# A fifth pair of split-weight buffers in place of two load buffers, and twelve unread products behind the router's logits

## The chip, the cores and the metric
The program runs on one core of one Trainium2 chip. The metric is the time of one execution on the device in microseconds (us). The engines that matter here are TensorE (PE in the profile; its weight loads are a row of their own, PEld), VectorE (DVE), ScalarE (ACT) and the queue of SyncE (SPq) that issues every transfer.

## The reference, cut to what matters
A trunk of two layers over 256 tokens of width 1024, all in float32. Layer 0 is a retention block and a dense SwiGLU block, layer 1 a pooling mixer and a block of eight experts. The change touches the way from the mixer through the router into the experts:

```python
logits = (xt @ w_router).astype(jnp.float32)
top_logits, top_idx = lax.top_k(logits, TOP_K)          # two of eight experts for each token
gates = jax.nn.softmax(top_logits, axis=-1)
...
(jax.nn.silu(h @ w_gate) * (h @ w_up)) @ w_down         # each expert: 1024 -> 3584 -> 1024
```

All eight experts' weights are read, 336 MiB in float32, whatever the router chooses.

## The kernel before, in words
Activations and weights stay in float32. A product is made from parts: a weight tile `w` is split into `w_hi` (the value rounded to float32r, written by ACT) and `w_lo` (the rest, `w - w_hi`, written by DVE), both by `split` at L118. An activation is split the same way. `mm3` (L166 to L168) adds three products of parts, `mm2` (L778, L779) two, for experts whose tokens fit in half a tile and whose activation parts lie side by side ("narrow" experts; the three "wide" ones use `mm3`).

**The tiles of weights.** A weight part is a tile of 128 x 2048 float32, 1 MiB. `load` (L144) takes the next load buffer from a ring of tags and issues one transfer on SyncE's queue. `halves_of` takes the next pair of buffers for `w_hi` and `w_lo`. A load buffer is free again when DVE has written `w_lo`; a pair is free again when PE has used it. Before the experts the kernel has three pairs. From the pool mixer on, a fourth is made of two buffers that served other tiles (tags `cb` and `T_l`). The ring in the experts' loop has six buffers of tag `raw` and four of tag `e8`; the `e8` buffers held `xT` and the four `yT` tiles of the retention block before, and join the ring at the start of the dense block. Two more (`SPARE`) help for a few loads at the start.

**The experts' loop.** Each expert has seven blocks of 512 hidden columns. `BLOCKS` puts the blocks of expert 0 first and mixes wide and narrow ones after that, three wide in each seven. `PROGRAM` lists the steps: for each block gate (`g`), up (`u`) and, two blocks later, down (`d`). A step uses two weight tiles, its first half the first and its second half the second: 24 products of 128 x 512 for a wide block, 16 for a narrow one. The loop stands inside `tc.manual_schedule()`: every engine gets its instructions in the order in which they are written. In that order each step splits two more tiles (`fetch`, one behind the step's products and one behind the small steps that follow), so that `AHEAD` tiles are split before their step:

```python
while len(stream) < AHEAD:
    fetch()
for n, (what, block) in enumerate(PROGRAM):
    ...
    ps = up(next_weights(), ready[p][0], not wide)
    fetch()
    ...
    step()
    fetch()
```

The split that stands behind a step's first half of products writes the pair which that half has just used, so ACT (and DVE behind it) waits there for PE. With every expert's last block come `scaled` (DVE, `y_g`, L848), `upper` (ACT, `yp`, L853), `lower` (DVE, `yp`, L858) and four products `give` (PE, L867) with an addition each (DVE, `xs`, L872); `give` and the gathers for the next expert (`prepare`, L753) write to two banks of PSUM (`tbank`) and wait for DVE to empty them.

**In front of the loop.** The router's logits are the last products of the mixer (L580). From them DVE makes `sel` (L602), PE three small sums (L648 to L650), DVE `slot` and the one-hot tiles `oh` (L730); PE gathers the first expert's tokens (L753), and ACT and DVE split them into `xe_n`. Only then can PE multiply by the first weights (L778).

Of the kernel before, what the change touches and what calls it, by code (L numbers as in the profile page):

```python
# [11 lines left out]
R = mybir.dt.float32r  # L12
# [7 lines left out]
P = 128  # L20
D = 1024
KD = D // P
T = 256
# [6 lines left out]
NE = 8  # L30
# [12 lines left out]

W_FIRST = (8, 4, 0, 2)
W_REST = (5, 9, 1, 3, 6, 10, 7, 11)
N_RAW, N_SPL, N_E8, N_OHT = 6, 3, 4, 4


HALF = P // 2
# [8 lines left out]
PROGRAM = [("d", BLOCKS[i - 2]) if what == "d" else (what, BLOCKS[i]) for i in range(NE * NJ + 2) for what in "gud"  # L58
           if (i > 1 if what == "d" else i < NE * NJ)]

AHEAD = 4
ALWAYS = math.inf

SPARE = ((8, "a8", 2, 2), (11, "kd", 1, 3))
# [5 lines left out]
def trunk(ctx, tc, x, cols, c_row, const, ada_0, ada, w_0, w_in, w_out, f_gu, f_dn, pool_w, m_g, m_u, m_d, out):  # L70
    nc = tc.nc
# [9 lines left out]
    def tbank():  # L81
        return psT.tile([P, 512], F, tag="t", name="tbank")

    def buf(tag, shape, bufs=1, dt=F, name=None):
        return act.tile([P] + shape, dt, tag=tag, name=name or tag, bufs=bufs)
# [24 lines left out]
    cb = buf("cb", [2048])[:, :D]  # L110
    silu_c = nc.scalar.activation(c1, c1, AF.Silu)
    for h in range(2):
        ps = tbank()
# [6 lines left out]
    @contextmanager  # L120
    def behind(*instructions):

        with ExitStack() as s:
            for i in instructions:
                s.enter_context(tc.issue_after(i.ins))
            yield


    ring = deque([("raw", N_RAW, ALWAYS)] * N_RAW)
    halves = deque([("w_hi", "w_lo", N_SPL)] * N_SPL)  # L130
# [138 lines left out]
    def tok(b):  # L269
        return slice(b * P, (b + 1) * P)  # L270
# [7 lines left out]
        normed(xn, b)  # L278
    hh, hl = hT_parts()
    a1 = cst.tile([P, KD], F, name="a1")  # L280
    xT = buf("e8", [KD, T], N_E8, name="xT")
    for b in range(TB):
        for g in range(0, KD, 4):
            ps = transpose4(xn[:, b, g * P:(g + 4) * P])
# [4 lines left out]
    for k in range(KD):  # L289
# [6 lines left out]
        for f in range(4):  # L296
            wh, wl = at(512 * f)
# [50 lines left out]
    def attend(h, st):  # L348
        s, vy = st[f"s{h}"], st[f"vy{h}"]
        v, y = vy[:, 0], vy[:, 1]  # L350
        yT = st[f"yT{h}"] = buf("e8", [2, 4, T], N_E8, R, name="yT")
        os = []
        mv = sm.tile([P, TB, 2], F, tag="mv", name="mv")
        for b in range(TB):
            o = bank()
            nc.tensor.matmul(o, s[:, tok(b)], v[:, 0], start=True, stop=(b == 0))
            if b:
                nc.tensor.matmul(o, s[:, 256:384], v[:, 1], start=False, stop=True)
            bn = sm.tile([P, 6], F, tag="bn", name="bn")
            nc.vector.bn_stats(bn, o)  # L360
            nc.vector.bn_aggr(mv[:, b], bn)
            nc.vector.scalar_tensor_tensor(y[:, b], o, mv[:, b, 0:1], y[:, b], op0=ALU.subtract, op1=ALU.mult)
        rs, _ = rstd_of(mv[:, :, 1], 1.0, TB)
        for b in range(TB):
            nc.scalar.activation(y[:, b], y[:, b], AF.Copy, scale=rs[:, b:b + 1])
            ps = transpose4(y[:, b])
            for i in range(4):
                gain = col[:, C_GN + 4 * h + i:C_GN + 4 * h + i + 1]
                p1, hi = ps[:, i * P:(i + 1) * P], yT[:, 0, i, tok(b)]
                nc.scalar.activation(hi, p1, AF.Copy, scale=gain)  # L370
                nc.vector.scalar_tensor_tensor(yT[:, 1, i, tok(b)], p1, gain, hi.bitcast(F),
                                               op0=ALU.mult, op1=ALU.subtract)
# [7 lines left out]
    st = {}  # L380
# [5 lines left out]
    for i, f in enumerate(W_REST):  # L386
        at = weights(w_in[i])
        pss = [bank() for _ in range(TB)]
        for k in range(KD):
            wh, wl = at(512 * k)  # L390
# [8 lines left out]
    for h in range(NH):  # L399
        yT = st[f"yT{h}"]  # L400
        at = weights(w_out[h])
        last = h == NH - 1
# [3 lines left out]
        for i, b in steps:  # L406
            for n in range(2):
                wh, wl = at(1024 * i + 512 * n)
# [1 line left out]
        ada_next(ADA_O[h])  # L410


    ring.extend([("e8", N_E8, ALWAYS)] * N_E8)
    xn = buf("a8", [TB, D], 2, name="xn")
    hh, hl = hT_parts()
    a = acol(0, 3, gain_of(0, 1))
# [2 lines left out]
    for b in range(TB):  # L419
        root, scaled, _ = normed(xn, b)  # L420
# [8 lines left out]
        for g in range(0, KD, 4):  # L429
            ps = transpose4(xn[:, b, g * P:(g + 4) * P])  # L430
            for i in range(4):
                k = g + i
# [38 lines left out]
    for j in range(NFB):  # L471
# [8 lines left out]
        if j == 7:  # L480
# [5 lines left out]
            r = buf("qk", [2, D], name="pool_rows")  # L486
            gs_row, gsb_row = row(r[:, 0], gs), row(r[:, 1], gsb)
            a_p, s_p = acol(1, 0, gain_of(1, 0)), mcol(1, 0)
        if j == 9:
# [4 lines left out]
            rt = cst.tile([P, KD, NE], F, name="rt")  # L494
            nc.vector.tensor_mul(rt, rt0, a_m.rearrange("p (k o) -> p k o", o=1).to_broadcast([P, KD, NE]))
            ps = tbank()
            for k in range(KD):
                nc.tensor.matmul(ps[:, 0:NE], s_m[:, k:k + 1].to_broadcast([P, P]), rt0[:, k],
                                 start=(k == 0), stop=(k == KD - 1))
# [3 lines left out]
    last = [(NFB - 2, down_weights(NFB - 2), th)]  # L503
# [8 lines left out]
    for b in range(TB):  # L512
        for j, at, th in last:
            for c in range(2):
                down_block(j, at, th, c, b)


    xn = buf("T_l", [TB, D], name="xn_p")
    hT = buf("a8", [TB, KD, P], 2, name="hT_p")
# [8 lines left out]
    r = buf("raw", [2, D], N_RAW, name="m_rows")  # L528
# [3 lines left out]
    xT = []  # L532
# [17 lines left out]
    for b in range(TB):  # L550
        pooled = [bank() for _ in range(2)]
        for g in range(0, KD, 4):
            ps = transpose4(xn[:, b, g * P:(g + 4) * P])
# [6 lines left out]
        for n in range(2):  # L560
            ps = bank()
# [14 lines left out]
    for b in range(TB):  # L576
        rs, root = norm_scale(b, lambda n: w2([512], "junk"))
        ps = tbank()
        for k in range(KD):
            nc.tensor.matmul(ps[:, 0:NE], xT[b][:, k], rt[:, k], start=(k == 0), stop=(k == KD - 1))  # L580
        nc.vector.scalar_tensor_tensor(lg[:, b], ps[:, 0:NE], rs, lg0, op0=ALU.mult, op1=ALU.add)
        if b == 0:

            for c in (slice(0, 512), slice(512, 1024)):
                nc.vector.scalar_tensor_tensor(xm[:, b, c], xm[:, b, c], rs, sm_row[:, c], op0=ALU.mult, op1=ALU.add)
# [31 lines left out]

    halves.append(("cb", "T_l", 1))  # L620
    once = [ring[i][:2] + (1,) for i in range(2)]
    ring.rotate(-2)
    for place, *spare in SPARE:
# [13 lines left out]
    def next_weights():  # L637
# [4 lines left out]
            return hi[:, c % 2048:c % 2048 + n], lo[:, c % 2048:c % 2048 + n]  # L642
        return at


    ps = tbank()
    tri = kp[:, K_TRI:K_TRI + P]
# [282 lines left out]
    with tc.manual_schedule():  # L930
# [3 lines that stand above are left out]
# [17 lines left out]
            else:  # L951
# [3 lines left out]
                ps = up(next_weights(), ready[p][0], not wide)  # L955
# [25 lines left out]
    place_i, _, room, most_i = known  # L981
# [120 lines left out]
```

## Time and profile before

| | us |
|---|---|
| median of three executions | 1387.05 (1383.2 to 1388.51) |
| the profiled execution, its own time | 1383.0 |
| the span of its profile | 1381.0 |
| PE busy in it | 1307.7 (95%) |
| DVE busy | 1214.6 (88%) |
| ACT busy | 957.5 (69%) |

The page counts an engine as busy while one of its instructions runs. Matmuls are pipelined and their ends are modelled: a product of 512 columns counts 0.39 us though the next one may start 0.23 us after it. So a gap in PE's busy time is a real stall, while a stall of less than 0.17 us is not seen as one. "Idle before" with a name behind an arrow is the time in which the engine stood still and what released it.

### The profile page before, as it was taken

The numbers are of one execution on the slowest core, as the hardware profiler recorded it, in microseconds if no ns is written. First come the engines' busy times: TensorE is split into PE (matmuls) and PEld (weight loads), VectorE is DVE, ScalarE is ACT, GpSimd is POOL, SyncE is SP. The second block draws the span as 40 slices with busy tenths as digits, with TensorE's granted clock in tenths as the row PEclk, the third lists the DMA queues.
The fourth block names the chain that finished last, engine by engine and source line by source line (L and its number), as shares of the span: only waits on it lengthen the run. The fifth ranks groups of instructions, "written<-read, shape, count | busy, mean of one in ns | idle before, by whom it ended". The sixth has DMA issues, their size and how long they took to land.

```text
span 1381.0 us, 16731 instructions
## 1 busy us (share of the span) xinstructions
PE 1307.7 (95%) x6142; PEld 1067.0 (77%) x6142; DVE 1214.6 (88%) x1119; ACT 957.5 (69%) x888; POOL 0.2 (0%) x4
## 2 busy tenths in 40 slices
PE   7999998999998889999999999999999999999994
PEld 5787877888887768877878877788778787878883
DVE  6889866998766799999989999999899889999994
ACT  6655455443436588877878887878877877878882
POOL 0000000000000000000000000000000000000000
PEclk9999999999999799999999999999999999999997
DMA  9977885898770999999999999999999999999950
GB/s 389 361 279 259 324 291 208 336 393 352 289 327 31 340 350 389 360 374 392 425 411 395 426 394 363 387 397 406 409 357 421 355 376 376 380 398 401 426 245 33
DMA packets 66474, 477.30 MB, mean 346 GB/s; under 512 B 7377, under 2 KB 7761, under 8 KB 8658
## 3 DMA queue, kind: packets, MB, share of 16 engines
q1 hardware_dynamic: 66386, 476.17, 87.9%
q8 instruction: 50, 0.82, 0.2%
q14 instruction: 38, 0.31, 0.1%
HBM read 475.10 MB, written 1.05 MB: 345 GB/s over the span
## 4 chain that ended last, share of the span: by engine, by line
PE 42%; DVE 13%; issue 7%; ACT 3%; DVEq 0%; ACTq 0%
DVE w_lo L118 10%; PE bank L779 8%; PE bank L778 8%; PE bank L166 7%; PE bank L167 7%; PE bank L168 6%; PE tbank L818 3%; ACT w_hi L118 2%; PE tbank L753 2%; PE tbank L867 1%; DVE xs L872 1%; DVE dT L118 1%; DVE yp L858 1%; DVE y_g L848 0%; DVE moe_h L798 0%
## 5 line engine op out<-in xcount | busy, mean ns | idle before, releaser
L118 DVE TENSOR_TENSOR w_lo<-raw,w_hi 128x2048 fp32r<-128x2048 f32 (+1 forms) x413 | 904.9, 2223 | 99.4 <-ACT w_hi L118 97.8
L118 ACT ACTIVATE w_hi<-raw 128x2048 fp32r<-128x2048 f32 (+1 forms) x413 | 757.8, 1864 | 188.8 <-PE bank L168 139.6
L779 PE MATMUL bank<-w_lo,xe_n 128*128 128x512 f32 x560 | 223.6, 399 | 6.7 <-DVE w_lo L118 5.7
L778 PE MATMUL bank<-w_hi,xe_n 128*128 128x512 f32 x560 | 224.5, 401 | 0.3 <-ACT w_hi L118 0.3
L166 PE MATMUL bank<-w_hi,T_h 128*128 128x512 f32 x352 | 141.3, 403 | 3.1 <-ACT T_h L118 3.1
L167 PE MATMUL bank<-w_lo,T_h 128*128 128x512 f32 x352 | 139.3, 396 | 2.4 <-DVE w_lo L118 2.4
L168 PE MATMUL bank<-w_hi,T_l 128*128 128x512 f32 x352 | 139.5, 397 | 0.5 <-DVE T_l L118 0.5
L779 PEld LDWEIGHTS bank<-w_lo,xe_n 128*128 128x128 f32 x560 | 106.8, 191 | 35.9 <-DVE w_lo L118 14.4
L166 PE MATMUL bank<-w_hi,xe 128*128 128x512 f32 x336 | 132.8, 395 | 0.0
L167 PE MATMUL bank<-w_lo,xe 128*128 128x512 f32 x336 | 131.8, 392 | 0.4
L168 PE MATMUL bank<-w_hi,xe 128*128 128x512 f32 x336 | 131.1, 390 | 0.0
L778 PEld LDWEIGHTS bank<-w_hi,xe_n 128*128 128x128 f32 x560 | 106.9, 191 | 22.2 <-ACT w_hi L118 0.8
L779 PE MATMUL bank<-w_lo,dT 128*128 128x512 f32 x280 | 112.3, 401 | 8.2 <-DVE w_lo L118 8.2
L778 PE MATMUL bank<-w_hi,dT 128*128 128x512 f32 x280 | 111.6, 398 | 6.4 <-DVE dT L118 6.4
L177 DVE SCALAR_TENSOR_TENSOR raw<-raw,cb 128x1024 f32<-128x1024 f32 x96 | 114.3, 1217 | 0.1
L166 PE MATMUL bank<-w_hi,dT 128*128 128x512 f32 x256 | 100.0, 391 | 0.0
L167 PE MATMUL bank<-w_lo,dT 128*128 128x512 f32 x256 | 99.7, 390 | 0.0
L168 PE MATMUL bank<-w_hi,dT 128*128 128x512 f32 x256 | 99.7, 390 | 0.0
L166 PEld LDWEIGHTS bank<-w_hi,T_h 128*128 128x128 f32 x352 | 67.2, 191 | 17.7 <-ACT T_h L118 3.8
L167 PEld LDWEIGHTS bank<-w_lo,T_h 128*128 128x128 f32 x352 | 67.1, 191 | 16.8 <-DVE w_lo L118 2.8
L168 PEld LDWEIGHTS bank<-w_hi,T_l 128*128 128x128 f32 x352 | 67.1, 190 | 15.2 <-DVE T_l L118 1.2
L167 PEld LDWEIGHTS bank<-w_lo,xe 128*128 128x128 f32 x336 | 63.1, 188 | 16.2 <-DVE w_lo L118 3.7
(227 smaller groups left out, 1415.0 us busy)
## 6 DMA issues: line engine op xcount, KB each, us to landing
raw<-in_m_g_dram SPq DMA_DIRECT2D x112, 1024.0 KB, 7.6
raw<-in_m_u_dram SPq DMA_DIRECT2D x112, 1024.0 KB, 7.6
raw<-in_m_d_dram SPq DMA_DIRECT2D x112, 1024.0 KB, 7.5
raw<-in_ada_dram SPq DMA_DIRECT2D x48, 1024.0 KB, 7.1
raw<-in_f_gu_dram SPq DMA_DIRECT2D x22, 1024.0 KB, 5.8
raw<-in_w_in_dram SPq DMA_DIRECT2D x16, 1024.0 KB, 5.1
raw<-in_f_dn_dram SPq DMA_DIRECT2D x11, 1024.0 KB, 6.9
raw<-in_w_dram SPq DMA_DIRECT2D x8, 1024.0 KB, 7.7
```

The source lines that it names most:

```text
L118: return nc.scalar.activation(hi, src, AF.Copy), nc.vector.tensor_sub(lo, src, hi.bitcast(F))
L166: nc.tensor.matmul(ps, xh, wh, start=start, stop=False)
L167: nc.tensor.matmul(ps, xh, wl, start=False, stop=False)
L168: nc.tensor.matmul(ps, xl, wh, start=False, stop=stop)
L177: nc.vector.scalar_tensor_tensor(s, s, 1.0, cb, op0=ALU.mult, op1=ALU.mult, accum_out=mod[:, m:m + 1])
L753: nc.tensor.matmul(ps[:, i * ns:(i + 1) * ns], xm[:, b, c], oh[:, b, 0:ns], start=(b == 0), stop=(b == TB - 1))
L778: nc.tensor.matmul(ps, x, wh, start=start, stop=False)
L779: nc.tensor.matmul(ps, x, wl, start=False, stop=stop)
L818: nc.tensor.matmul(ps[:, i, c], a[:, c * P:(c + 1) * P], fold, start=True, stop=True)
L858: nc.vector.tensor_sub(yp[:, 1, half(n)], y_g[:, half(n)], yp[:, 0, half(n)].bitcast(F))
L867: nc.tensor.matmul(ps, ohT[:, tok(b)], yp[:, i, half(n)], start=(i == 0), stop=(i == 1))
L872: nc.vector.scalar_tensor_tensor(xs[:, b, c], st.pop("ps"), gates[b], xs[:, b, c], op0=ALU.mult, op1=ALU.add)
```

## The change
Two of the four `e8` buffers become a tag of their own, `f8`, with the same total size. Until the dense block ends they do what they did: `xT` and two of the four `yT` tiles lie in them, then they are load buffers. In front of the experts' loop the change takes them out of the ring (eight load buffers stay) and makes a fifth pair of them, and `AHEAD` goes from four to five. Beside that, twelve products of 128 x 512 are written behind the last of the logits' products. They multiply the first 512 columns of the last dense down part's `w_hi` (`last_at`) by 128 of the same columns into a bank that nobody reads.

```diff
--- before.py
+++ after.py
@@ -43,7 +43,7 @@
 
 W_FIRST = (8, 4, 0, 2)
 W_REST = (5, 9, 1, 3, 6, 10, 7, 11)
-N_RAW, N_SPL, N_E8, N_OHT = 6, 3, 4, 4
+N_RAW, N_SPL, N_E8, N_OHT = 6, 3, 2, 4
 
 
 HALF = P // 2
@@ -58,7 +58,7 @@
 PROGRAM = [("d", BLOCKS[i - 2]) if what == "d" else (what, BLOCKS[i]) for i in range(NE * NJ + 2) for what in "gud"
            if (i > 1 if what == "d" else i < NE * NJ)]
 
-AHEAD = 4
+AHEAD = 5
 ALWAYS = math.inf
 
 SPARE = ((8, "a8", 2, 2), (11, "kd", 1, 3))
@@ -278,7 +278,7 @@
         normed(xn, b)
     hh, hl = hT_parts()
     a1 = cst.tile([P, KD], F, name="a1")
-    xT = buf("e8", [KD, T], N_E8, name="xT")
+    xT = buf("f8", [KD, T], N_E8, name="xT")
     for b in range(TB):
         for g in range(0, KD, 4):
             ps = transpose4(xn[:, b, g * P:(g + 4) * P])
@@ -348,7 +348,7 @@
     def attend(h, st):
         s, vy = st[f"s{h}"], st[f"vy{h}"]
         v, y = vy[:, 0], vy[:, 1]
-        yT = st[f"yT{h}"] = buf("e8", [2, 4, T], N_E8, R, name="yT")
+        yT = st[f"yT{h}"] = buf("e8" if h % 2 else "f8", [2, 4, T], N_E8, R, name="yT")
         os = []
         mv = sm.tile([P, TB, 2], F, tag="mv", name="mv")
         for b in range(TB):
@@ -410,7 +410,7 @@
         ada_next(ADA_O[h])
 
 
-    ring.extend([("e8", N_E8, ALWAYS)] * N_E8)
+    ring.extend([(tag, N_E8, ALWAYS) for tag in ("e8", "f8") for _ in range(N_E8)])
     xn = buf("a8", [TB, D], 2, name="xn")
     hh, hl = hT_parts()
     a = acol(0, 3, gain_of(0, 1))
@@ -514,6 +514,8 @@
             for c in range(2):
                 down_block(j, at, th, c, b)
 
+    last_at = last[-1][1]
+
 
     xn = buf("T_l", [TB, D], name="xn_p")
     hT = buf("a8", [TB, KD, P], 2, name="hT_p")
@@ -577,7 +579,7 @@
         rs, root = norm_scale(b, lambda n: w2([512], "junk"))
         ps = tbank()
         for k in range(KD):
-            nc.tensor.matmul(ps[:, 0:NE], xT[b][:, k], rt[:, k], start=(k == 0), stop=(k == KD - 1))
+            logits = nc.tensor.matmul(ps[:, 0:NE], xT[b][:, k], rt[:, k], start=(k == 0), stop=(k == KD - 1))
         nc.vector.scalar_tensor_tensor(lg[:, b], ps[:, 0:NE], rs, lg0, op0=ALU.mult, op1=ALU.add)
         if b == 0:
 
@@ -617,7 +619,8 @@
 
 
 
-    halves.append(("cb", "T_l", 1))
+    ring = deque(r for r in ring if r[0] != "f8")
+    halves.extend([("f8", "f8", N_E8), ("cb", "T_l", 1)])
     once = [ring[i][:2] + (1,) for i in range(2)]
     ring.rotate(-2)
     for place, *spare in SPARE:
@@ -642,6 +645,12 @@
             return hi[:, c % 2048:c % 2048 + n], lo[:, c % 2048:c % 2048 + n]
         return at
 
+
+    ps = tbank()
+    wh, _ = last_at(0)
+    with behind(logits):
+        for _ in range(12):
+            nc.tensor.matmul(ps, wh[:, 0:P], wh, start=True, stop=True)
 
     ps = tbank()
     tri = kp[:, K_TRI:K_TRI + P]
```

The order of instructions, at the three places that the prediction speaks of. First PE, behind the logits (`rt,xT_r` are the router and the turned tokens; `sel` the chosen experts), before:

```order
L580 MATMUL tbank<-rt,xT_r 128x8 x16
L648 MATMUL tbank<-sel,kp 128x8
L649 MATMUL tbank<-sel,kp 128x8
L650 MATMUL tbank<-sel,one 128x8
L753 MATMUL tbank<-oh,xm 128x64 x16
```

and with the change:

```order
L582 MATMUL tbank<-rt,xT_r 128x8 x16
L653 MATMUL tbank<-w_hi 128x512 x12
L657 MATMUL tbank<-sel,kp 128x8
L658 MATMUL tbank<-sel,kp 128x8
L659 MATMUL tbank<-sel,one 128x8
L762 MATMUL tbank<-oh,xm 128x64 x16
```

The twelve products stand between the logits and the small sums over `sel`, on which all of the routing hangs. Second DVE, from the first two tiles' splits (in halves of 1024) to the gating (`mx`), before:

```order
L730 TENSOR_SCALAR oh<-kp,slot,sel 128x128 x2
L118 TENSOR_TENSOR w_lo<-raw,w_hi 128x1024 x2
L118 TENSOR_TENSOR xe_n<-tbank,xe_n 128x4x64 x2
L118 TENSOR_TENSOR w_lo<-raw,w_hi 128x2048 x5
L657 TENSOR_REDUCE mx<-lg 128x2
```

and with the change:

```order
L739 TENSOR_SCALAR oh<-kp,slot,sel 128x128 x2
L118 TENSOR_TENSOR w_lo<-raw,w_hi 128x1024 x2
L118 TENSOR_TENSOR xe_n<-tbank,xe_n 128x4x64
L118 TENSOR_TENSOR w_lo<-raw,w_hi 128x2048
L118 TENSOR_TENSOR xe_n<-tbank,xe_n 128x4x64
L118 TENSOR_TENSOR w_lo<-raw,w_hi 128x2048 x5
L666 TENSOR_REDUCE mx<-lg 128x2
```

One split of a whole tile now stands between the two halves of `xe_n`, and one more in all ahead of `mx`; ACT's `w_hi` stand in the same way. Third DVE, at the end of the loop, before:

```order
L118 TENSOR_TENSOR w_lo<-raw,w_hi 128x2048 x2
L848 TENSOR_TENSOR y_g<-bank,g_row 128x512 x2
L118 TENSOR_TENSOR w_lo<-raw,w_hi 128x2048
L858 TENSOR_TENSOR yp<-y_g,yp 128x512 x2
L822 TENSOR_TENSOR h_n<-tbank,sg_n 128x256
L118 TENSOR_TENSOR dT<-h_n,dT 128x4x64
```

and with the change:

```order
L118 TENSOR_TENSOR w_lo<-raw,w_hi 128x2048 x2
L857 TENSOR_TENSOR y_g<-bank,g_row 128x512 x2
L867 TENSOR_TENSOR yp<-y_g,yp 128x512 x2
L831 TENSOR_TENSOR h_n<-tbank,sg_n 128x256
L118 TENSOR_TENSOR dT<-h_n,dT 128x4x64
```

The last tile's split no longer stands between `y_g` and `yp`, but earlier, ahead of the earlier rows. On SyncE's queue the loads of the experts keep their order; at the start of the dense block two loads of conditioning weights and two of the dense block change places.

## Rows read from the trace of the kernel before
**Rows 1.** Busy time by stretch (us, busy and count per engine, PEclk, DMA, GB/s)
```profile
459.44:562.00 102.56, 93.53 (x464) 76.62 (x463) 95.10 (x91) 84.94 (x73) 0.00 (x0) 0.96 0.95 359
1008.30:1126.50 118.20, 111.72 (x559) 93.26 (x558) 109.50 (x74) 91.89 (x72) 0.00 (x0) 1.00 0.98 378
sum 887.86, PE 853.40 PEld 701.67 DVE 834.68 ACT 712.51 POOL 0.00; mean PE 106.67 PEld 87.71 DVE 104.33 ACT 89.06 POOL 0.00
```

**Rows 2.** Waits from 459 to 1347 us: engine, line, releaser; total, times, longest
```profile
ACT w_hi L118 <- PE bank L168: 55.4, 63, 2.4
DVE w_lo L118 <- ACT w_hi L118: 48.3, 57, 2.5
PEld bank L779 <- DVE w_lo L118: 28.4, 36, 2.3
PE bank L779 <- DVE w_lo L118: 13.8, 14, 1.9
PE tbank L867 <- DVE xs L872: 10.7, 7, 2.9
```

**Rows 3.** Groups of instructions, 500 to 1340 us, the two halves of a split
```profile
L118 DVE TENSOR_TENSOR w_lo<-raw,w_hi 128x2048 fp32r<-128x2048 f32 x317 | 711.8, 2284 | 45.1 <-ACT w_hi L118 43.8
L118 ACT ACTIVATE w_hi<-raw 128x2048 fp32r<-128x2048 f32 x317 | 596.3, 1915 | 92.8 <-PE bank L168 55.4 <-PE bank L778 24.4 <-ACT dT L118 8.5
```

**Rows 4.** Waits of SyncE's DMA queue, 459 to 1347 us
```profile
SPq L144 <- DVE w_lo L118: 599.3, 275, 6.9
```

**Rows 5.** Timeline at an expert's end: start, us, engine, instruction, idle before it
```profile
1093.89 1.23 ACT L853 ACTIVATE yp<-y_g 128x512 fp32r<-128x512 f32 x2 [2.96 <-DVE y_g L848]
1096.96 4.50 DVE L118 TENSOR_TENSOR w_lo<-raw,w_hi 128x2048 fp32r<-128x2048 f32 x2 [2.50 <-ACT w_hi L118]
1097.19 0.40 PE L779 MATMUL bank<-w_lo,xe_n 128*128 128x512 f32 x1
1097.42 0.39 PE L778 MATMUL bank<-w_hi,xe_n 128*128 128x512 f32 x1
1099.31 0.50 PE L779 MATMUL bank<-w_lo,xe_n 128*128 128x512 f32 x1 [1.50 <-DVE w_lo L118]
```

**Rows 6.** Waits from 562 to 1347 us, behind expert 0
```profile
PE bank L779 <- DVE w_lo L118: 9.5, 10, 1.9
```

**Rows 7.** The page's DMA issues: instruction, count, size, median us to landing
```profile
raw<-in_m_g_dram SPq DMA_DIRECT2D x112, 1024.0 KB, 7.6
```

**Rows 8.** Busy time by stretch, one of 20 us
```profile
680.00:700.00 20.00, 19.56 (x90) 15.77 (x89) 18.36 (x12) 18.23 (x14) 0.00 (x0) 1.00 1.01 427
```

**Rows 9.** Timeline from the router's logits to the first expert's products
```profile
441.62 5.30 PE L580 MATMUL tbank<-rt,xT_r 128*128 128x8 f32 x32
449.17 0.60 PE L648 MATMUL tbank<-sel,kp 128*128 128x8 f32 x2 [2.24 <-DVE sel L602]
452.27 7.09 PE L753 MATMUL tbank<-oh,xm 128*128 128x64 f32 x32 [1.66 <-DVE oh L730]
459.82 0.42 DVE L118 TENSOR_TENSOR xe_n<-tbank,xe_n 128x256 fp32r<-128x256 f32 x1 [2.56 <-ACT xe_n L118]
```

**Rows 10.** Timeline of the loop's last blocks
```profile
1346.97 1.28 DVE L848 TENSOR_TENSOR y_g<-bank,g_row 128x512 f32<-128x512 f32 x2
1350.75 2.29 DVE L118 TENSOR_TENSOR w_lo<-raw,w_hi 128x2048 fp32r<-128x2048 f32 x1 [2.50 <-ACT w_hi L118]
1355.54 0.80 PE L778 MATMUL bank<-w_hi,dT 128*128 128x512 f32 x1 [6.37 <-DVE dT L118]
1356.13 0.63 PE L779 MATMUL bank<-w_lo,dT 128*128 128x512 f32 x1
1356.56 0.63 PE L778 MATMUL bank<-w_hi,dT 128*128 128x512 f32 x1
```

**Rows 11.** Busy time by stretch, the gathers and the first weight products
```profile
456.00:460.00 4.00, 4.00 (x19) 3.92 (x19) 0.61 (x2) 0.94 (x3) 0.00 (x0) 0.50 0.99 371
464.00:466.00 2.00, 2.00 (x10) 1.60 (x10) 1.88 (x2) 1.31 (x3) 0.00 (x0) 1.00 0.85 328
```

## The prediction
> **What bounds the kernel now.** I read the busy times by stretch first, because the change works from 440 us on and almost all of it in the experts' loop. From PE's first weight product (459.44 us) to the last block but one (1347.3) the loop takes 887.9 us. PE is busy for 853.4 of them, DVE for 834.7 and ACT for 712.5 [rows 1]. So two engines are nearly full, with 34 and 53 us to spare, and neither alone is the bound. In expert 0, where all blocks are narrow, DVE is the busier (95.1 of 102.6 us, PE 93.5). In a later round of seven blocks PE is (111.7 of 118.2, DVE 109.5) [rows 1]. A wide block costs PE 72 products and a narrow one 48, while DVE splits six tiles for either, so the two engines take turns in waiting.
>
> Second I read the waits. ACT's `w_hi` waits for PE's last product on a pair (55.4 us with wide blocks alone), DVE's `w_lo` waits for `w_hi` (48.3), and PE waits for `w_lo`: 28.4 us as seen by its weight loads and 13.8 as seen by its products [rows 2]. That is a ring: a used pair, ACT 1.92 us, DVE 2.28 us, PE again [rows 3]. No row says that `w_hi` waits for a transfer; SyncE's queue instead waits 599 us for `w_lo` to free a load buffer [rows 4]. So the pairs are the scarce buffers and the load buffers are not.
>
> Third I read one expert's end in the timeline. ACT stands 2.96 us because its next instruction, `yp`, needs DVE's `y_g`, which needs PE's last down product. The next `w_hi` is queued behind `yp`, DVE's next split starts only at 1096.96 after 2.50 us of idle time, and PE runs out of parts: the product after the one at 1097.42 starts at 1099.31 (1.50 us idle) [rows 5].
>
> **The fifth pair in the loop.** It moves nothing relative to a pair's release: the split behind a step's first half still writes the pair of that half. But the tile is now one further ahead, so PE may run one tile longer before it needs it. The longest wait for `w_lo` is 2.3 us [rows 2], and a split costs DVE 2.28 [rows 3]: one tile of reserve covers every single one. What comes back is between nothing and 28.4 us. Nothing, because DVE's other work does not get earlier: where PE no longer waits for `w_lo` it may wait as much longer in the next `give` (10.7 us now [rows 2]). 28.4, if no wait moves. I take **9.5 us**: what PE's products show behind expert 0 [rows 6]. The other 4.3 of the 13.8 lie in expert 0, where DVE is the bound and no reserve makes it faster. I stay at the products' row because the weight loads run ahead of them, so that part of their 28.4 is hidden.
>
> **Two load buffers fewer.** A split runs every 2.65 us (317 in 840 us [rows 3]), so ten buffers come round in 26.5 us and eight in 21.2. A buffer is used for 7.6 us by its transfer [rows 7] and 1.92 + 2.28 by the split [rows 3], 11.8 in all. A landed tile now waits about 14.7 us, and would wait 9.4. These are estimates from those rows. The cost is **0**; the cover is the 9.4 us. Two fewer tiles also lie ready before the routing, which the same reserve covers.
>
> The Trainium skill speaks against that, in "DMA: Bandwidth & Descriptors", Specifications: it gives about 358 GB/s as the limit of HBM for one core, at which 352 MB would take 984 us (an estimate by the page) and no pair could help. The trace disagrees: it holds 427 GB/s over 20 us [rows 8].
>
> **The twelve products.** The logits end at 446.9 us (441.62 + 5.30), and PE then stands 2.24 us until `sel` is there at 449.17 [rows 9]. Twelve products issue every 0.23 us at the full clock (1097.19 to 1097.42 [rows 5]) or every 0.43 at the lower one (1356.13 to 1356.56 [rows 10]), so they take 2.8 to 5.2 us. They end at 449.7 to 452.1 and delay the sums over `sel` by 0.5 to 2.9 us. Behind those sums are `slot`, `oh`, the gathers, `xe_n` and every first product. ACT's third `w_hi` waits too, since it rewrites the tile that they read; it has a hole until `xe_n` to make that up.
>
> What they may give back is the clock. During the gathers the granted clock is 0.50, the lower of its two levels (1.2 GHz), with PE busy all the time; it is 1.00 only from 464 us [rows 11]. The gathers take 7.09 us [rows 9] and would take about half at 2.4 GHz; the first nine weight products lose about 0.2 us each. So 3.5 + 1.8 us is the most.
>
> I do not expect all of it. Gathers alone, with PE busy throughout 456 to 460 us, did not raise the clock [rows 11], so it may fall again during them. The skill's rule ("TensorE: Matmul & The Clock Gate", What's actually happening) is that the default is throttled and activity releases it; taken alone, it would give the whole 5.3 us.
>
> DVE also puts one split between the two halves of `xe_n`, where it idles 2.56 us now [rows 9]: 2.28 us of work for nothing, and DVE is the bound up to about 560. Against that stands the delay. From +2.9 with nothing back to -5.3 + 0.5 - 2.3 = -7.1, I take **0**: the row nearest is the gathers' own, which argues that the clock is not kept.
>
> **The loop's end.** DVE finishes `y_g` at 1348.25, idles 2.50 us for the last `w_hi`, splits until 1353.0 and only then makes `yp`, `h_n` and `dT`, for which PE waits 6.37 us [rows 10]. The last split now stands ahead of `y_g`. Its 2.29 us remain, since DVE is full before it, but the idle time goes, except about a microsecond in which `yp` needs ACT: **-2 us**, between -1.2 and -4.8 (idle time and split).
>
> **The start of the dense block.** The four `yT` buffers come free in another order, and two of SyncE's loads change places with two others. PE does not wait for weights there; **0**, with that cover.
>
> **The sum** is -9.5 - 2 + 0 + 0 = -11.5 us against the profiled execution's 1383.0 us (span 1381.0): 1371.5. That execution is 4 us below the median of 1387.05, from which the forecast is 1375.5, rounded to 1375.
>
> **Rivals.** *Waits only move.* If DVE's other work (`give`, gathers, gating) sets the pace in each round, the waits for `w_lo` reappear at `tbank`. Then only the tail is left, with the start between +2.9 and 0: 1387 - 2 + 1 = 1386. For it speaks that DVE has 95.1 of 102.6 us in expert 0 [rows 1]; against it, its 53 us of idle time elsewhere. Chance 0.26.
>
> *All of it comes back.* No wait moves and the clock is kept: -28.4 - 4.8 and up to -5: some 1352 to 1358. The two engines take turns in waiting, which speaks for it; but DVE would be left with 25 us of slack in 888, which rounds that swing by several us do not allow. Chance 0.12.
>
> *Eight load buffers are too few* (slower). A tile waits in its buffer 9.4 us on average. Should the transfer take not 7.6 but more than 17 us (7.6 + 9.4), each round of the ring lasts longer than 21.2 us, and SyncE's queue, which issues in order, passes it on to all loads behind. At 18 us a tile costs (18 + 4.2)/8 = 2.78 us in place of 2.65; over half the loop's 336 tiles that is +22 us, less what the pair gives: about 1398. The 427 GB/s stretch speaks against it, since 1.05 MB there takes 2.5 us. Chance 0.06.
>
> *The transfers set the pace already*: the DMA share is 0.95 to 1.01 in the rows [rows 1, 8]. But 352 MB at 427 GB/s take 825 us, 63 less than the loop. If so, nothing changes: 1386. Chance 0.04.
>
> **Chances and range.** The forecast (7 to 18 us gained) has 0.52. A measurement of this kernel can tell about 0.5%, 7 us, from no change. Faster by more: 0.52 + 0.12 and a little of the first rival, 0.67. The same: the rest of that rival and the fourth, 0.26. Slower: 0.07. The range goes from 1359, most of the case in which all comes back, to 1388, the case in which waits move with the start at its worst; the slower rival stays outside.
>
> **What would show it.** Right: PE's waits for `w_lo` fall below a third, ACT's waits for PE at `w_hi` remain, and PE's waits at L867 grow by less than that; the last down block starts within about 4 us of the folds. The clock's rows around the gathers tell which way the twelve products went, and the sums over `sel` stand 0.5 to 2.9 us further behind the logits. Wrong: PE's waits at `tbank` take over what `w_lo` loses; or `w_hi` waits for transfers, with SyncE's waits for `w_lo` longer than now.

## The result and the profile after

The changed kernel takes 1392.89 us (median of 14 runs, 1391.1 to 1397.74), the kernel before 1386.47 (14 runs, 1383.2 to 1391.15). The ratio is 1.0059, 95% interval 1.0047 to 1.0072: **slower by 0.6%**, where 1375 was forecast.

| | before | after |
|---|---|---|
| span of the profiled execution, us | 1381.0 | 1390.2 |
| its own time, us | 1383.0 | 1391.97 |
| mean granted clock of TensorE | 0.982 | 0.971 |
| PE's first weight product to its last, us | 459.44 to 1361.83 = 902.4 | 458.99 to 1371.12 = 912.1 |

All of the loss lies in the experts' loop: +9.7 us between the two profiled executions, which lie 9.0 us apart where the medians lie 6.4 apart. The loop starts half a microsecond earlier than before, because the logits end 1.5 us earlier in this execution. The lines of the kernel after stand nine further down (L778 is L787 now, L779 L788, L753 L762, L867 L876, L872 L881; L166 to L168 have not moved).

**Waits.** The waits of the kernel after from 459 to 1357 us (engine, line, releaser; total, times, longest):

```profile
DVE w_lo L118 <- ACT w_hi L118: 58.4, 60, 2.9
ACT w_hi L118 <- PE bank L168: 48.7, 45, 4.6
ACT w_hi L118 <- PE bank L787: 35.9, 17, 5.2
...
PE tbank L876 <- DVE xs L881: 15.0, 8, 3.5
...
PE tbank L876 <- DVE yp L867: 7.0, 3, 4.2
...
PE tbank L762 <- DVE oh L739: 6.4, 2, 4.7
...
PEld bank L788 <- DVE w_lo L118: 5.2, 7, 1.9
...
PE tbank L762 <- DVE oh L743: 3.5, 1, 3.5
...
PE bank L788 <- DVE w_lo L118: 2.4, 2, 1.5
...
DVE w_lo L118 <- DMA raw<-in_m_u_dram: 1.4, 1, 1.4
...
DVE w_lo L118 <- DMA raw<-in_m_d_dram: 0.5, 1, 0.5
```

From the same list of the kernel before:

```profile
ACT g_out L810 <- PE bank L779: 5.8, 8, 1.7
...
PE tbank L753 <- DVE oh L730: 1.3, 2, 0.7
...
PE tbank L753 <- DVE oh L734: 1.0, 1, 1.0
```

Against [rows 2], PE's waits for `w_lo` fell from 28.4 to 5.2 us (weight loads) and from 13.8 to 2.4 (products). Its waits at `tbank` rose: for `xs` from 10.7 to 15.0, for `oh` from 2.3 to 9.9 (6.4 + 3.5), and for `yp` from nothing to 7.0. They are few and long, up to 4.7 us. Transfers are waited for during 1.9 us in the whole loop.

**One such place.** The timeline of the kernel after at the expert's end that [rows 5] show before (start, duration, engine, line, operation; in brackets the idle time before it and its releaser):

```profile
1111.27 0.40 PE L788 MATMUL bank<-w_lo,dT 128*128 128x512 f32 x1
1111.45 4.49 DVE L118 TENSOR_TENSOR w_lo<-raw,w_hi 128x2048 fp32r<-128x2048 f32 x2
...
1115.85 0.60 DVE L739 TENSOR_SCALAR oh<-kp,slot_p,sel_p 128x128 f32<-128x128 f32 x2
...
1116.34 3.65 PE L762 MATMUL tbank<-oh,xm 128*128 128x64 f32 x16 [4.67 <-DVE oh L739]
...
1119.75 0.77 PE L787 MATMUL bank<-w_hi,xe_n 128*128 128x512 f32 x1
...
1120.32 0.63 PE L788 MATMUL bank<-w_lo,xe_n 128*128 128x512 f32 x1
...
1120.74 0.63 PE L787 MATMUL bank<-w_hi,xe_n 128*128 128x512 f32 x1
```

Before, PE ran out of parts inside its steps here: the products at 1099.31 [rows 5] and 1105.52 start 1.66 and 2.04 us late. Now the parts are there and PE gets through. It then needs `oh`, which stands on DVE behind two splits (4.49 us) of tiles that PE doesn't need yet, and waits 4.67 us in one piece. After it products start every 0.42 us instead of every 0.23.

**The clock.** The busy time by stretch (us; busy and count of PE, PEld, DVE, ACT, POOL; granted clock; DMA share; GB/s) for that wait, the gathers behind it and the products behind those, and ahead of them the round of seven blocks that [rows 1] show before:

```profile
1015.00:1138.70 123.70, 116.88 (x560) 97.87 (x559) 108.25 (x73) 92.00 (x72) 0.00 (x0) 0.94 0.95 357
...
1111.50:1116.30 4.80, 0.17 (x1) 0.00 (x0) 4.80 (x5) 4.80 (x5) 0.00 (x0) 0.84 0.92 316
1116.30:1119.70 3.40, 3.36 (x16) 3.39 (x17) 3.40 (x3) 1.15 (x1) 0.00 (x0) 0.50 1.00 402
1119.70:1125.00 5.30, 5.30 (x14) 4.15 (x14) 3.69 (x3) 2.27 (x2) 0.00 (x0) 0.50 0.97 373
```

TensorE ran at 0.50, the lower of its two levels (1.2 GHz), through the gathers and at least 14 products. The round as a whole is 5.50 us longer than before (118.20 in [rows 1]), and PE's idle time in it is not: 118.20 - 111.72 = 6.5 us before, 123.70 - 116.88 = 6.8 after. What grew is the busy time of the same work, by 5.2 us, with the granted clock down from 1.00 to 0.94. From 470 to 1340 us the record of the clock holds 6.8 us at the lower level before and 47.8 after, in ten stretches. The loop without its last blocks, before and after:

```profile
459.44:1347.30 887.86, 853.40 (x4105) 701.67 (x4104) 834.68 (x555) 712.51 (x551) 0.00 (x0) 0.99 0.97 383
...
458.99:1356.60 897.61, 857.39 (x4087) 715.52 (x4086) 830.56 (x554) 711.00 (x551) 0.00 (x0) 0.97 0.97 382
```

In the other runs of the kernel after, time and clock go together too: the five of 1396.6 us or more have a mean clock of 0.967, the profiled one 0.971.

**A count of the waits.** From one product's start to the next I took off the time that a product takes at the full clock in these traces: 0.228 us at 512 columns, 0.112 for the smaller ones. What is left is a gap. A product at the lower clock leaves one of about 0.2 us without any wait. From 470 us to the loop's last product the gaps add up to, in us:

| | before | after |
|---|---|---|
| gaps of over 0.25 us (how many) | 48.3 (44) | 48.5 (28) |
| smaller gaps behind products at the lower clock | 5.0 | 21.2 |
| smaller gaps behind products at the full clock | 8.4 | 2.0 |

The long waits only moved: they have the same sum, in fewer and longer pieces. The short waits at the full clock are 6.5 us less, which is what the fifth pair brought (1.5 us in e2, which has the pair, and 7.9 and 9.5 in e1 and e3, which do not). The slow products at the lower clock cost 16.2 us more. The difference, 9.7 us, is the loop's loss.

**The start.** The timeline of the kernel after behind the logits:

```profile
445.30 4.58 PE L653 MATMUL tbank<-w_hi 128*128 128x512 f32 x12
...
447.47 0.17 DVE L604 TENSOR_SCALAR sel<-sel 128x16 f32<-128x16 f32 x1
...
449.73 0.29 PE L657 MATMUL tbank<-sel,kp 128*128 128x8 f32 x2
...
452.21 6.71 PE L762 MATMUL tbank<-oh,xm 128*128 128x64 f32 x32 [1.75 <-DVE oh L739]
```

The busy times and the granted clock there, by stretch:

```profile
445.80:449.20 3.40, 3.40 (x9) 2.66 (x9) 2.91 (x7) 0.34 (x1) 0.00 (x0) 0.50 0.53 125
449.20:452.60 3.40, 1.65 (x13) 1.46 (x12) 2.10 (x5) 2.68 (x2) 0.00 (x0) 1.00 0.43 183
452.60:458.90 6.30, 6.30 (x32) 6.30 (x31) 4.51 (x4) 3.22 (x3) 0.00 (x0) 0.50 0.98 342
```

The twelve products delay the sums over `sel` by 2.1 us (`sel` is ready at 447.64). They did raise the clock (e2, without them, has 0.50 from 445.1 to 458.7), but for the 3.40 us in which PE mostly waited for `slot` and `oh`. In the gathers it was 0.50 again.

**The loop's end**, in the kernel after:

```profile
1360.86 1.28 DVE L857 TENSOR_TENSOR y_g<-bank,g_row 128x512 f32<-128x512 f32 x2
...
1362.24 1.29 DVE L867 TENSOR_TENSOR yp<-y_g,yp 128x512 fp32r<-128x512 f32 x2
...
1364.83 0.80 PE L787 MATMUL bank<-w_hi,dT 128*128 128x512 f32 x1 [2.44 <-DVE dT L118]
```

The split between `y_g` and `yp` is gone, and PE waits 2.44 us for `dT` in place of 6.37 [rows 10].

### The profile page after: what moved, and what is told of

Same layout as the page of the kernel before. It is cut to its first block, busy times and chain, and to the rows that moved or that the text cites. A ratio compares the mean times of both kernels' runs of the same rounds, so it can differ in the third digit from the quotient of the medians.

```text
span 1390.2 us, 16750 instructions
## 1 busy us (share of the span) xinstructions
PE 1317.1 (95%) x6154; PEld 1084.3 (78%) x6154; DVE 1215.1 (87%) x1119; ACT 956.1 (69%) x888; POOL 0.2 (0%) x4
## 5 line engine op out<-in xcount | busy, mean ns | idle before, releaser
L787 PE MATMUL bank<-w_hi,xe_n 128*128 128x512 f32 x560 | 229.2, 409 | 0.0
L788 PE MATMUL bank<-w_lo,xe_n 128*128 128x512 f32 x560 | 225.5, 403 | 1.6 <-DVE w_lo L118 1.5
L166 PE MATMUL bank<-w_hi,T_h 128*128 128x512 f32 x352 | 140.9, 401 | 3.1 <-ACT T_h L118 3.1
L168 PE MATMUL bank<-w_hi,T_l 128*128 128x512 f32 x352 | 139.3, 396 | 0.6 <-DVE T_l L118 0.5
L166 PE MATMUL bank<-w_hi,xe 128*128 128x512 f32 x336 | 134.3, 400 | 0.0
L168 PE MATMUL bank<-w_hi,xe 128*128 128x512 f32 x336 | 132.5, 394 | 0.0
L788 PEld LDWEIGHTS bank<-w_lo,xe_n 128*128 128x128 f32 x560 | 109.7, 196 | 25.6 <-DVE w_lo L118 2.7
L787 PEld LDWEIGHTS bank<-w_hi,xe_n 128*128 128x128 f32 x560 | 110.3, 197 | 23.2
L787 PE MATMUL bank<-w_hi,dT 128*128 128x512 f32 x280 | 111.4, 398 | 2.4 <-DVE dT L118 2.4
L788 PE MATMUL bank<-w_lo,dT 128*128 128x512 f32 x280 | 111.0, 397 | 1.0 <-DVE w_lo L118 0.9
L166 PE MATMUL bank<-w_hi,dT 128*128 128x512 f32 x256 | 100.8, 394 | 0.0
L168 PE MATMUL bank<-w_hi,dT 128*128 128x512 f32 x256 | 100.7, 393 | 0.0
L166 PEld LDWEIGHTS bank<-w_hi,T_h 128*128 128x128 f32 x352 | 67.0, 190 | 17.6 <-ACT T_h L118 3.7
L168 PEld LDWEIGHTS bank<-w_hi,T_l 128*128 128x128 f32 x352 | 66.9, 190 | 15.4 <-DVE T_l L118 1.5
L168 PEld LDWEIGHTS bank<-w_hi,xe 128*128 128x128 f32 x336 | 63.9, 190 | 13.9
```

The lines of the kernel that those rows point to most:

```text
L166: nc.tensor.matmul(ps, xh, wh, start=start, stop=False)
L168: nc.tensor.matmul(ps, xl, wh, start=False, stop=stop)
L787: nc.tensor.matmul(ps, x, wh, start=start, stop=False)
L788: nc.tensor.matmul(ps, x, wl, start=False, stop=stop)
```

## The experiments

The theory after these readings: the fifth pair did what was forecast, but `AHEAD = 5` lets PE run one tile further ahead of DVE, so its waits gather at `tbank` behind splits that it does not need yet, and behind those long waits the clock falls. Rivals: the twelve products, the two missing load buffers, the long waits as such. "Loop" is the time from PE's first weight product to its last in the profiled execution, "half clock" what the record holds at the lower level from 470 to 1340 us. Ratios are to the kernel before on the same chip, with 95% intervals.

| run | pairs | AHEAD | twelve products | loop, us | half clock, us | ratio |
|---|---|---|---|---|---|---|
| before | 4 | 4 | no | 902.4 | 6.8 | 1 |
| after | 5 | 5 | yes | 912.1 | 47.8 | 1.0059 [1.0047, 1.0072] |
| e1_products | 4 | 4 | yes | 903.8 | 13.7 | 1.0003 [0.9981, 1.0025] |
| e2_pair_no_products | 5 | 5 | no | 913.2 | 53.6 | 1.0023 [1.0004, 1.0042] |
| e3_eight_load_buffers | 4 | 4 | no | 903.9 | 13.7 | 0.9993 [0.9980, 1.0007] |
| e4_pair_ahead_4 | 5 | 4 | yes | 893.3 | 13.7 | 0.9929 [0.9903, 0.9955] |
| e5_filled_gaps | 5 | 5 | yes | 891.7 | 3.4 | 0.9899 [0.9867, 0.9931] |
| e6_ahead_4_tail_5 | 5 | 4, then 5 | yes | 890.6 | 6.8 | 0.9895 [0.9860, 0.9930] |
| e7_four_pairs_ahead_3 | 4 | 3 | no | 935.6 | 16.0 | 1.0214 [1.0182, 1.0247] |
| e8_pair_ahead_3 | 5 | 3 | yes | 936.0 | 10.2 | 1.0234 [1.0201, 1.0266] |
| e9_before_filled | 4 | 4 | no | 901.8 | 6.8 | 0.9992 [0.9982, 1.0003] |
| e10_ahead_4_tail_5_filled | 5 | 4, then 5 | yes | 889.8 | 6.8 | 0.9908 [0.9890, 0.9926] |
| e11_ahead_5_filled_more | 5 | 5 | yes | 891.0 | 0 | 0.9906 [0.9889, 0.9923] |
| e12_ahead_5_filled_no_products | 5 | 5 | no | 887.5 | 0 | 0.9883 [0.9865, 0.9900] |

### Which part costs: e1, e2, e3

**e1_products**: the kernel before with the product block alone.

> The kernel before with the twelve products alone (four pairs, ten load buffers, AHEAD 4). The theory: the loss sits in the experts' loop. PE gets one tile further ahead of DVE, its many short waits for w_lo become a few waits of 2 to 5 us at the tbank (oh, yp, xs), and behind each of these the granted clock falls to one half; the products have no part in it. So here: 1384 to 1389 us, ratio 0.998 to 1.002, at most 10 us of half clock behind 470 us. Rival P (the products shift the start by some us and all that follows falls out of step): about 1393 us, ratio 1.004 or more.

**e2_pair_no_products**: the kernel after without it.

```diff
-    ps = tbank()
-    wh, _ = last_at(0)
-    with behind(logits):
-        for _ in range(12):
-            nc.tensor.matmul(ps, wh[:, 0:P], wh, start=True, stop=True)
```

> The changed kernel without the twelve products (five pairs, eight load buffers, AHEAD 5). The theory: the whole loss is here, 1391 to 1397 us, ratio 1.004 to 1.008, with 30 to 55 us of half clock behind 470 us and PE's waits at the tbank as in the changed kernel (about 27 us from start to start at the gives). Rival P: 1385 to 1388 us, ratio 1.000.

**e3_eight_load_buffers**: `f8` leaves the ring and nothing is made of it.

```diff
-AHEAD = 5
+AHEAD = 4
...
-    halves.extend([("f8", "f8", N_E8), ("cb", "T_l", 1)])
+    halves.append(("cb", "T_l", 1))
```

(The products are out as in e2.)

> Two load buffers left out and nothing else: eight load buffers, four pairs, AHEAD 4, no products. The theory: ratio 0.998 to 1.002, some 1386 us, PE's waits for w_lo as in the kernel before (28 us by the weight loads), hardly any half clock in the loop. Rival L (the loss comes from the load buffers, late transfers): ratio 1.004 or more, with waits of w_hi or w_lo for transfers of over 5 us.

Two load buffers fewer cost nothing that can be seen (0.9993), nor do the products with four pairs (1.0003). The loop of e2 is 1.1 us longer than the changed kernel's, with 53.6 us of half clock: what costs is the pair with its `AHEAD`. e2's ratio, 1.0023, lies below its forecast of 1.004 and below the changed kernel's 1.0059, and the two intervals do not meet, so the products do cost a little: from the last logit to the first weight product it is 12.8 to 12.9 us in the six profiles of the table without them, and 13.4 to 14.3 in the eight with them. e1 and e3 have two falls of the clock more than the kernel before (13.7 us at half clock, where I had put 10 at most), and their loops are 1.4 and 1.5 us longer.

### How far ahead: e4, e7, e8

**e4_pair_ahead_4**: five pairs, splits written as far ahead as before.

```diff
-AHEAD = 5
+AHEAD = 4
```

> The changed kernel with AHEAD 4: five pairs, but each split written as far ahead as in the kernel before, so that one pair is free and ACT need not wait for the step's own products. The theory: DVE's other work stands where it stood and DVE may run ahead, so PE's waits for w_lo stay small, those at the tbank go back to the kernel before's (15 us at the gives from start to start) or below, and the clock holds: 1370 to 1384 us, ratio 0.988 to 0.998. Rival F (any fifth pair brings PE's waits together, wherever the splits stand): 1391 to 1396 us as in the changed kernel. Rival L: also about 1393 us.

The loop takes 893.3 us, 18.8 less than the changed kernel's and 9.1 less than before. Waits of e4 from 459 to 1345 us:

```profile
ACT g_out L819 <- PE bank L788: 50.1, 27, 3.8
DVE w_lo L118 <- ACT w_hi L118: 43.0, 40, 2.5
...
PEld bank L788 <- DVE w_lo L118: 22.7, 27, 2.3
...
PE bank L788 <- DVE w_lo L118: 11.9, 12, 1.9
...
ACT w_hi L118 <- PE bank L168: 9.8, 13, 1.0
...
PE tbank L876 <- DVE xs L881: 9.0, 7, 2.9
...
PE tbank L762 <- DVE oh L739: 0.7, 1, 0.7
```

One pair is always free here, so ACT's `w_hi` waits for PE's wide products for 9.8 us in place of 55.4 [rows 2]. ACT itself waits no less: it now stands at what comes behind the splits, above all at `g_out` (50.1 us, 5.8 before). But the splits are made earlier. DVE waits for `w_hi` for 43.0 us in place of 48.3 [rows 2], and PE's waits for `w_lo` and at `tbank` both fall a little. By the count above the long gaps fall from 48.3 us to 41.5 and the smaller ones from 13.4 to 12.5, of which 7.2 are at the lower clock (5.0 before): against the kernel before, e4 gains by waits and not by the clock. At the same expert's end, e4's timeline:

```profile
1097.29 4.49 DVE L118 TENSOR_TENSOR w_lo<-raw,w_hi 128x2048 fp32r<-128x2048 f32 x2
...
1099.63 0.50 PE L788 MATMUL bank<-w_lo,dT 128*128 128x512 f32 x1 [1.89 <-DVE w_lo L118]
...
1101.70 0.60 DVE L739 TENSOR_SCALAR oh<-kp,slot_p,sel_p 128x128 f32<-128x128 f32 x2
...
1102.34 2.50 PE L762 MATMUL tbank<-oh,xm 128*128 128x64 f32 x16
```

`oh` stands behind two splits here as well. But PE needs the first of them inside its own step (idle for 1.89 us, at 1099.63), has products to do behind it, and goes into the gather without a wait. The clock is not spared altogether. It fell behind the 1.89 us too, for 3.4 us in place of the 10.2 in the kernel after:

```profile
1099.90:1103.30 3.40, 3.40 (x13) 2.68 (x12) 3.40 (x4) 3.40 (x2) 0.00 (x0) 0.54 0.82 267
```

**e7_four_pairs_ahead_3** and **e8_pair_ahead_3**: `AHEAD = 3` in the kernel before and in the kernel after.

> The kernel before with AHEAD 3: four pairs, one of them free. The theory says that both count: how far ahead the splits are written (which sets how long PE can run when DVE does its other work) and a free pair (which lets ACT and DVE run before PE is done). With splits only three ahead PE's waits for w_lo grow beyond the 28 us of the weight loads to 45 or more, while the waits at the tbank shrink below 15 us: 1390 to 1405 us, ratio 1.003 to 1.014. Rival G (a free pair is all that counts, the place of the splits is not): 1374 to 1380 us, ratio 0.991 to 0.996.

> Five pairs and AHEAD 3, two pairs free. The theory: splits stand as in the run with four pairs and AHEAD 3, so PE's waits for w_lo grow again, and the second free pair adds little because ACT already waits for hardly any product with one free (9.8 us): 1378 to 1395 us, above the 1375.6 of AHEAD 4. Rival G (the more pairs free, the better): 1368 to 1375 us.

Both take 2% more, and e7 more than expected (1414.62 us). From e7's waits, 460 to 1395 us:

```profile
PEld bank L779 <- DVE w_lo L118: 67.2, 87, 2.1
```

From e8's, in the same stretch:

```profile
PEld bank L788 <- DVE w_lo L118: 68.5, 88, 2.1
```

With three tiles ahead PE waits for `w_lo` more than twice as often as before (36 times [rows 2]). A fifth pair changes nothing in that. That a free pair is all that counts is thus refuted, and so is my own expectation for e8, 1378 to 1395 us: it took 1418.37. The clock hardly falls in either (16.0 and 10.2 us at the lower level); this loss is made of waits, with long gaps of 62.9 and 67.9 us where the kernel before has 48.3.

### The clock by itself: e5, e9

**e5_filled_gaps**: unread products ahead of eleven of PE's waits.

```diff
+FILL = {12: 14, 31: 6, 45: 6, 64: 7, 70: 11, 106: 8, 120: 18, 127: 9, 142: 14}
+FILL_D = {26: 7, 101: 16}
...
+    def keep(ps, n):
+        for _ in range(n):
+            nc.tensor.matmul(ps[:, 0:P], ident, xm[:, 0, 0:P], start=True, stop=True)
...
+            if n in FILL:
+                spare_bank = bank()
+                keep(spare_bank, FILL[n])
+            if n in FILL_D:
+                filled.append(FILL_D[n])
             step()
```

(`spare_bank` is the bank of the next step's products, which start it anew; with `FILL_D` the next `give` calls `keep` on its own bank.)

> The changed kernel with unread products of 128 x 128 in float32 (109 in eleven places) put on PE ahead of the gathers and gives that waited 1.9 to 4.8 us in its profile; nobody else waits for them. The theory: PE's waits have only moved (single waits of over 0.25 us sum up to 51.6 us from 470 us on before and 51.9 after), and the 6 us are the slow products behind each long wait (47.8 us at half clock from 470 to 1360 us, 17.1 before). With the waits filled the clock should hold: at most 25 us of half clock, 1381 to 1388 us, ratio 0.996 to 1.001. Rival S (the long waits themselves are the loss, the clock is a by-product): 1390 us or more, ratio 1.003 or more, whatever the clock does.

(The edit has 116 such products, not 109: nine places with 93, two with 23. The 51.6 and 51.9 us run beyond the loop's last product, at which the count above ends.) The loop fell by 20.4 us, to 891.7, more than expected. The same place in e5, PE's timeline (each unread product has two records, so 36 are 18):

```profile
1099.92 4.18 PE L850 MATMUL bank<-xm,kp 128*128 128x128 f32 x36
1104.75 1.52 PE L764 MATMUL tbank<-oh,xm 128*128 128x64 f32 x12 [0.65 <-DVE oh L741]
```

DVE's timeline:

```profile
1099.86 4.49 DVE L120 TENSOR_TENSOR w_lo<-raw,w_hi 128x2048 fp32r<-128x2048 f32 x2
1104.26 0.60 DVE L741 TENSOR_SCALAR oh<-kp,slot_p,sel_p 128x128 f32<-128x128 f32 x2
```

The busy times of the round and of the stretch behind the wait:

```profile
1005.22:1123.19 117.97, 116.95 (x611) 99.40 (x610) 109.88 (x74) 92.05 (x72) 0.00 (x0) 1.00 0.97 381
...
1105.00:1110.00 5.00, 5.00 (x31) 4.43 (x31) 5.00 (x3) 2.84 (x3) 0.00 (x0) 1.00 1.00 360
```

`oh` comes 4.4 us after the splits begin, as in the kernel after, and PE's useful work resumes no earlier for it. But the clock is 1.00 behind it. From 470 to 1340 us 44.4 us of half clock are gone. In the count above, with the unread products left out, the long gaps between PE's useful products are 46.4 us, 2.1 less than in the kernel after, and the smaller ones 4.9, which is 18.2 less. So nine tenths of the 20.4 us came from the clock. Rival S falls: PE's useful work waits nearly as long in e5, and it is the clock behind the waits that was lost.

**e9_before_filled**: the same in the kernel before, at its own waits (`FILL = {12: 4, 64: 7, 70: 11, 106: 9, 127: 9, 142: 6}`).

> The kernel before with 46 such unread products ahead of its own waits at the tbank (1.2 to 3.2 us in six places). Its profile shows only 3.4 us of half clock in the loop behind 480 us and 10.2 at its very end, so by the theory there is little to win back: 1382 to 1387 us, ratio 0.997 to 1.000. Rival B (unread products help by themselves, with or without a fall of the clock): 1377 us or less, ratio 0.993 or less.

0.9992: where the clock did not fall, filling brings nothing.

### Towards a faster kernel: e6, e10, e11, e12

**e6_ahead_4_tail_5**: e4, and one tile more near the end.

```diff
             step()
             fetch()
+            if n == 160:
+                fetch()
```

> Five pairs with AHEAD 4, and one more tile split behind step 160 of 168, so that only the loop's end has its splits five ahead. The theory: the last wait of PE for dT falls from 6.6 to some 2.7 us as in the changed kernel, nothing else moves: 1370 to 1373 us, ratio 0.987 to 0.991. Rival: the extra split delays the last gives or folds by as much: 1375 to 1378 us.

In the two timelines the last wait for `dT` falls by 6.37 - 2.58 = 3.8 us; the loop as a whole is 2.8 us shorter than e4's. The ratios of e4 and e6 overlap, so the gain is seen in the profiles alone.

**e10_ahead_4_tail_5_filled** (`FILL = {1: 14, 12: 4, 64: 6, 70: 11, 106: 6, 127: 6, 142: 6}`, `FILL_D = {101: 4}`), **e11_ahead_5_filled_more** (e5 and `{1: 14, 28: 4, 139: 4}`) and **e12_ahead_5_filled_no_products** (e11 without the twelve products).

> Five pairs, AHEAD 4, one more tile near the end, and 57 unread products ahead of its seven waits of 1.2 to 3.7 us. Its clock fell for 10.2 us only, so the theory gives 1 to 4 us: 1368 to 1372 us, ratio 0.986 to 0.990. Rival B: 1362 us or less.

> The run with filled gaps (AHEAD 5) and three more places filled: 14 products ahead of the sums over sel's counts behind step 1 (3.7 us, behind which the clock fell for 3.4 us) and 4 each behind steps 28 and 139. The theory: the half clock at 473 us goes, 1 to 2 us more than the 1372 before: 1368 to 1372 us, ratio 0.986 to 0.990. If the place does not matter, 1372 to 1374.

> The same without the twelve products behind the logits. The theory (they are worth nothing): within 2 us of the run beside it. Rival (the clock they lend to the first gathers is worth 3 us or more): 1372 to 1376 us.

e10 and e11 take the same time (1369.43 and 1369.5 us). With the waits filled, it does not matter here whether the splits stand four or five ahead. e12 is the fastest of all, 1367.04 us (1365.07 to 1367.61), 1.2% below the kernel before and, by the two ratios (0.9883 and 1.0059), 1.7% below the changed one. Its loop runs at full clock throughout:

```profile
456.53:1343.00 886.47, 874.65 (x4407) 737.31 (x4406) 836.63 (x561) 713.13 (x555) 0.00 (x0) 1.00 0.97 386
```

It beats e11 by 2.5 us in the medians, where I had expected 2 at most either way. Of that, 1.3 us are the way from the last logit to the first weight product (14.0 and 12.8 us), so the rival by which the products lend the gathers a useful clock falls. The rest stays open. In the profiles the loop is 3.5 us shorter as well: behind the last wait for `dT` (2.4 us in both) the clock falls in e11 and holds in e12.

## Why the prediction was wrong

**The fifth pair in the loop** is the step that failed: "What comes back is between nothing and 28.4 us". The lower end had its mechanism right: "where PE no longer waits for `w_lo` it may wait as much longer in the next `give`". That happened (48.3 us of long gaps before, 48.5 after). But I took an equal sum of waits for an equal time, and put the clock behind the waits at nothing without a reason. 44 gaps became 28 longer ones, the clock fell behind them, and the slow products cost 16.2 us more, against 6.5 us of short waits saved: the loop became 9.7 us longer. A loss had to be in the range, and *Waits only move* was priced at 1386 for want of it. The rows held a hint: a round whose clock was 1.00 [rows 1] beside products every 0.43 us behind the 6.37 us wait [rows 10]. I used those for the twelve products and not for the loop.

The Trainium skill names this loss: "TensorE: Matmul & The Clock Gate", in "HAM oscillation — how this bites in real kernels", tells of a kernel that waits between groups of products and pays for a cold start after each. The trace agrees: 0.50 behind the 4.67 us wait, 1.00 when it was filled. The prediction drew only on the other half of that rule, that activity releases the clock.

Where a fifth pair does gain, the sizes come near the forecast, and in e4 that is luck. It takes 9.1 us off the loop, against the forecast 9.5, but by a pair that is free before PE is done. The prediction saw, rightly, that `AHEAD = 5` leaves no such pair (it "moves nothing relative to a pair's release") and counted on one tile of reserve. With that reserve and the clock held the loop is 10.7 us shorter (e5), against 9.5 + 2. About 4 of them are the last wait for `dT`, so the pair gives some 7 us. What the text missed is that PE's reserve is also a distance from DVE's other work.

Two sums of the text don't come out. *All of it comes back* gives 1387 - 28.4 - 4.8 = 1354, and 1349 with the 5 us for the clock, not 1352 to 1358. And a range that starts at 1359 holds none of that case, where the text says most of it.

**The loop's end** was right in its mechanism and small in its size: -2 was forecast within -1.2 to -4.8, and PE's wait went from 6.37 to 2.44, 3.9 less. That is more than the 2.50 us of idle time, so part of the split's 2.29, which the text let remain, went too. In e6, which changes this step alone, the wait falls by 3.8 us.

**Two load buffers fewer** was right at 0 (e3: 0.9993), and the rival built on it fell: 1.9 us of waits for transfers.

**The twelve products**, forecast at 0 between -7.1 and +2.9, cost between 0.6 and 1.5 us on the way to the first weight product (13.4 to 14.3 against 12.8 to 12.9). The two terms that I weighed came as argued: the sums are 2.1 us late (0.5 to 2.9 forecast), and the clock fell again during the gathers, whose 6.71 us replace 7.09. The changed kernel against e2 and e11 against e12 show a cost in the time too; e1 against the kernel before shows none.

**What would show it**: PE's waits for `w_lo` fell below a third, and ACT's waits for PE at `w_hi` remained (48.7 + 35.9 us); both proved nothing about the time. The sign given for wrong, waits at `tbank` that take over what `w_lo` loses, is the one that came.

## What to carry to other kernels

A deeper buffer doesn't remove the wait for a second engine that is nearly full; it moves it to the next place where the two meet, and that place may be worse. Compare not only the sum of PE's waits but their lengths, and look at the granted clock behind each long one. When a change that should gain loses, put unread products into the long waits: if the time comes back, it was the clock, and a filled wait may be left in as the remedy.

How deep the buffers are and how far ahead the work is written are two settings. Here five pairs gained 10 us with the work four tiles ahead and nothing with it three ahead.

## What was not expected of the hardware

Waits of the same length did not always cost the clock. In the kernel after, ten of the twelve single gaps of 1.86 us or more that end between 470 and 1340 us go with a stretch of half clock; gaps of 2.17 and 3.11 us do not. In the kernel before, gaps of 2.14, 3.10, 2.49, 2.04 and 2.48 us left it at 1.00, and gaps of 3.69 and 2.10 did not. e2, without the products, falls at the same ten waits as the kernel after. But e3, whose gaps in the loop are those of the kernel before to a few hundredths, falls behind two of them (2.04 and 1.61 us) that left the clock at 1.00 there. So neither the length of a wait nor its place settles it. What decides was not tried and stays open. So the numbers of filling products, which were fitted to one profile, may need to be fitted again after any change.

Such falls are easily overlooked. The page of the kernel after, whose row of the clock has 40 slices, shows of the ten in the loop no more than an 8 in three slices:

```profile
PEclk9999999999999899999999999999989989999998
```

(The first 8 also holds the first gathers; the one at the right end is the loop's end and what follows.)
